# One encoder layer in float32 on one core: the level-16 update of a scan moved into its preparation, 20 column pairs ahead of the scan instead of 19, and another order of loads for the down projection

## The chip, the cores and the metric

The kernel runs on one core of a Trainium2 chip, in one launch. The metric is the device time of the whole program in microseconds (us). Five engines work side by side, each on a queue of its own: TensorE (PE in the profile; its loads of weights are PEld), VectorE (DVE), ScalarE (ACT), GpSimd (POOL) and SyncE (SP), which issues most of the DMA transfers. Matmuls write into PSUM, which holds eight banks of 128x512 float32.

## What is computed

One layer of a bidirectional encoder, batch 1, 1024 positions, model width 1024. The reference, cut to what matters here:

```
proj = einsum("bsd,de->bse", rmsnorm(x), w_in)
glu_in, q, v, z_f, z_b, og, g_a, g_b = split(proj)      # 1024 columns each
a = conv module on glu_in: glu, depthwise conv of 31, layernorm, silu, product with pw_w
o = gated scan forwards (q, v, z_f) + gated scan backwards (q, v, z_b)   # 8 heads of 128
b = (rmsnorm per head(o) * norm_w * silu(og)) @ o_w
x = x + (sigmoid(g_a) * a + sigmoid(g_b) * b) @ w_out
up, val = split(rmsnorm(x) @ w_up)                        # 2816 columns each
x = x + (silu(dwconv3(up)) * val) @ w_down
out = rmsnorm(x)
```

The scan of one head is S_t = diag(f_t) S_(t-1) + k_t v_t^T, o_t = S_t^T q_t, in float32, with f = lb + (1 - lb) sigmoid(z) and k = 1 - f.

## The kernel before

**Products.** Every product in float32 is made of three matmuls of two-part operands: the operand is copied to a rounded high part by ScalarE, the low part is the difference, by VectorE (`split`, L122 to L128), and `mm3` (L146 to L150) issues high x high, high x low, low x high. Weights come as raw tiles `wr` or `sw` and are split to `wp` or `wq`. A *standard job* (`std_job`) makes a column block of 128 for two halves of 512 positions; it gives control back after every six matmuls, one *piece*. A *pair job* (`pair_job`) takes two column blocks together as a 2x2 block product in seven products instead of eight, Winograd's form, with sums of weights and of activations made by VectorE or by adding DMAs; a pair has 14 pieces. Evictions `su` keep products for later sums; in the down projection they are made on L1805.

**Order.** TensorE's instructions run in the order in which the program issues them. For the other engines a planner that works with its own costs chooses the order, except for instructions that are pinned (`pin`), which stay in program order. DMA issues of SyncE stand in one queue, so a load whose tile is not free yet holds up the loads behind it. Streams of work are interleaved by hand: `fill(n)` issues n pieces of a stream, fractions being carried over.

**Ahead of the scan.** The first NPAIRS = 19 pairs of the 28 in the list `todo` (q, og, then v, z forwards and z backwards of each head, then the two gates) are pair jobs. They are issued between the 124 steps of the depthwise convolution (CONV_FILL pieces a step), then between the parts of the layer norm (fixed numbers of pieces), and what is left is drained. The columns that remain are standard jobs in the stream `dense`, with the product with pw_w behind them; their last pieces fill the scan.

**The scan** goes through 16 half heads (8 heads, two halves of 512 positions). Within 32 positions it works by levels of 1, 2, 4, 8 and 16: at each level the keys kG and the queries qF are copied out (`woven`, L1170 to L1175, ScalarE, into one of 8 rotating buffers `A`), and then kG and qF are multiplied in place by the decay of the level (`double_keys` and `double_queries`, through `tt` on L1142, VectorE), and the totals `tb` are combined. `scan_base` prepares a half head in five steps up to level 8, and copies out A16; its last step was empty. `scan_levels` then issues the matmuls of levels 8 and 16 into one bank (L1193; level 16 reads qF itself by a view of two runs of 16), doubles for 16, and merges the results into D by masked copies (L1294). Next come the blocks of 32 (L1276, behind a zeroing with `none`, L1298), the doubling for 32, the blocks of 64, and the copy of the result to S, onto which four DMAs from ScalarE's queue put D (L1306). `scan_states` turns kG (L1316), copies it out as kT (L1318, ScalarE) and multiplies it with v (L1325). `scan_outputs` of the head before runs meanwhile as `pending`.

After each of these five parts `between(FILL)` is called: FILL = 1.77 pieces of the dense stream, one step of the next half head's preparation, and one step of the pending outputs. That is 80 calls in all.

**The down projection** treats the first 6 column tiles of the gated activations by standard jobs (48 pieces), then 12 by two blocks of seven-product jobs, and the last 4 by standard jobs. Their tiles are loaded by `load_part` into seven landing tiles (`ev` and `tm`), issued on L1758, and split four pieces later into buffers of high and low parts (`hx` and `gx`), pinned. The first 12 loads come in the last pieces of the stage before. For the first seven-product block, 12 loads come early, and nine in the pieces -2 to +6 around its start; their buffers are those of the first tiles.

Of the kernel before, what the change touches and what calls it, by code (L numbers as in the profile page):

```python
# [16 lines left out]
AX = mybir.AxisListType  # L17

P = 128
FILL = 1.77  # L20
TAIL = ((1, 2), (1, 1), (2, 4), (2, 3))
CONV_FILL = 1.67
NPAIRS = 19
LN_FILL = 6
LN_LAST = 12
GLU_FIRST = 4
# [5 lines left out]
H = 512  # L32
# [5 lines left out]
def view(t, off, dims):  # L38

    return bass.AP(  # L40
        tensor=t.tensor,
        offset=t.offset + off,
        ap=[list(t.ap[0])] + [list(d) for d in dims],
    )
# [3 lines left out]
def tile_hybrid_encoder(  # L48
# [201 lines left out]
    def std_job(src, nk, acts, evac, halves=(0, 1), step=2):  # L250


        def prep():
            raw = raw_w(src, nk)
            return split(w_page(nk), w_page(nk), raw, V)

        def run(w, halves=halves):
            for half in halves:
                acc = bank("mm")
                for k in range(nk):  # L260
                    mm3(acc, w, acts(k, half), k, k == 0, k == nk - 1)
                    if k % step == step - 1 or k == nk - 1:
                        yield
                evac(half, acc)

        return prep, run
# [306 lines left out]
    FIRST, NS, SEVENS = 6, 3, 2  # L573
# [254 lines left out]
    def in_pair(n):  # L828
        (c0, e0), (c1, e1) = todo[2 * n], todo[2 * n + 1]
        evs = (e0, e1)  # L830
        return pair_job(
            in_cols(c0),
            in_cols(c1),
            NK2,
            lambda i: ht[i],
            p1,
            p1,
            lambda e, *quadrant: evs[e](*quadrant),
            first=n == 0 or n >= 14,
            columns=2,  # L840
        )
# [179 lines left out]

    jobs = collections.deque(in_pair(n) for n in range(1, NPAIRS))
    jobs.appendleft((lambda: w_pair0, pair0[1]))
# [20 lines left out]
    for _ in conv_steps():  # L1044
        s_pairs.fill(CONV_FILL)

# [39 lines left out]

    rest = todo[2 * NPAIRS :]
    rest_jobs = [std_job(in_cols(c), ND, h_std, e) for c, e in rest[:-2]]
# [78 lines left out]
    def pairs(t, h, other=H):  # L1167

        return view(t, 0, [[other + h, 2], [2 * h, H // (2 * h)], [1, h]])

    def woven(t, h):

        t_h = page(hp, "A", 8)
        A.copy(pairs(t_h, h, 0), pairs(t, h))  # L1174
        return t_h  # L1175

    def slot(b, n):
        return b[:, n * P : (n + 1) * P]
# [12 lines left out]
    def level(b, A_t, Q_t):  # L1191
        for at, g, o in each():
            T.matmul(b[g, o], A_t[:, at : at + 32], Q_t(at), start=True, stop=True)  # L1193

    def row(t):
        return lambda at: t[:, at : at + 32]

    def double_keys(kG, tb, h):
        n, nb = H // (2 * h), H // h
        tt(pairs(kG, h), pairs(kG, h), view(tb, 1, [[nb - 1, 2], [2, n], [0, h]]))  # L1200

    def double_queries(qF, q, tb, h):
        n, nb = H // (2 * h), H // h
        tt(pairs(qF, h), q, view(tb, nb + 1, [[-(nb + 1), 2], [2, n], [0, h]]))

    def totals(tb, h, to=None):
        n, nb = H // (2 * h), H // h
        tn = None
        if to is None:
            tn = hp.tile([P, 2, n], F32, tag=f"tb{h}", name=nm("tb"), bufs=1 if h < 8 else 2)  # L1210
            to = view(tn, 0, [[n, 2], [1, n]])
        tt(to, view(tb, 0, [[nb, 2], [2, n]]), view(tb, 1, [[nb, 2], [2, n]]))
        return tn

    def scan_base(ins):


        q, f, kG, ks = ins
        qF = hp.tile([P, 2, H], F32, tag="qF", name=nm("qF"), bufs=4)
        D_t = hp.tile([P, 4, 32], F32, tag="D", name=nm("D"), bufs=3)  # L1220
        for d in range(2):
            V.tensor_scalar(kG[:, d, :], kG[:, d, :], ks[:, d : d + 1], None, op0=ALU.mult)
        k_d, Q1 = page(hp, "A", 8), page(hp, "A", 8)
        tt(k_d, kG[:, 0, :], kG[:, 1, :], ALU.add)
        A1 = woven(kG, 1)
        odd = H // 2
        tt(
            pairs(Q1, 1, 0),
            view(q, 0, [[1, 2], [2, odd], [1, 1]]),
            view(f, H, [[1 - H, 2], [2, odd], [1, 1]]),  # L1230
        )
        tt(
            view(qF, 1, [[H - 1, 2], [2, odd]]),
            view(q, 1, [[-1, 2], [2, odd]]),
            view(f, H + 1, [[-(H + 1), 2], [2, odd]]),
        )
        double_keys(kG, f, 1)
        double_queries(qF, pairs(Q1, 1, 0), f, 1)
        tb = totals(f, 1)
        yield  # L1240
        A2, Q2 = woven(kG, 2), woven(qF, 2)
        double_keys(kG, tb, 2)
        double_queries(qF, pairs(qF, 2), tb, 2)
        tb = totals(tb, 2)
        A4, Q4 = woven(kG, 4), woven(qF, 4)
        yield
        b = bank("sc")
        for n, (k_t, q_t) in enumerate(((k_d, q), (A1, Q1), (A2, Q2), (A4, Q4))):
            level(slot(b, n), k_t, row(q_t))
        double_keys(kG, tb, 4)  # L1250
        double_queries(qF, pairs(qF, 4), tb, 4)
        tb = totals(tb, 4)
        A8, Q8 = woven(kG, 8), woven(qF, 8)
        yield
        A.copy(D_t, near(slot(b, 3)))
        for n, m in enumerate((m_d, m_1, m_2)):
            V.copy_predicated(D_t, over(m), near(slot(b, n)))
        double_keys(kG, tb, 8)
        double_queries(qF, pairs(qF, 8), tb, 8)
        tb = totals(tb, 8)  # L1260
        A16 = woven(kG, 16)
        yield
        yield qF, kG, tb, D_t, A8, Q8, A16

    def scan_levels(base, S_t, Tt):


        qF, kG, tb, D_t, A8, Q8, A16 = base

        def blocks(b, h):  # L1270

            for c in range(0, H, P):
                for s0 in range(0, P, h):
                    t0 = s0 ^ h
                    d = s0 // h % 2
                    T.matmul(  # L1276
                        b[s0 : s0 + h, c + t0 : c + t0 + h],
                        kG[:, d, c + s0 : c + s0 + h],
                        qF[:, 1 - d, c + t0 : c + t0 + h],
                        start=True,  # L1280
                        stop=True,
                    )

        def double(tb, h, to=None):
            double_keys(kG, tb, h)
            double_queries(qF, pairs(qF, h), tb, h)
            return totals(tb, h, to)

        b = bank("ob")
        level(slot(b, 0), A8, row(Q8))  # L1290
        level(slot(b, 1), A16, lambda at: view(qF, at, [[H + 16, 2], [1, 16]]))
        tb = double(tb, 16)
        for n, m in enumerate((m_8, m_16)):
            V.copy_predicated(D_t, over(m), near(slot(b, n)))  # L1294
        yield
        b = bank("sc")
        for at, g, _ in each():
            T.matmul(b[g, at : at + 32], none, none, start=True, stop=True)  # L1298
        blocks(b, 32)
        tb = double(tb, 32)  # L1300
        yield
        blocks(b, 64)
        double(tb, 64, view(Tt, 0, [[4, 2], [1, 4]]))
        A.copy(S_t, c4(b))
        for g in range(0, P, 32):
            nc.scalar.dma_start(S_t[g : g + 32, :, g : g + 32], D_t[g : g + 32])  # L1306
        yield
# [135 lines left out]
    for h in range(NH):  # L1443
# [4 lines left out]
        for half in range(2):  # L1448
            i = 2 * h + half
            base = cur.result()  # L1450
# [11 lines left out]
            for n, _ in enumerate(scan_levels(base, S_t, Tt[:, half])):  # L1462
                if n == 1:
                    b = bank("tr")
# [3 lines left out]
                    A.copy(v.rearrange("p c e -> p (c e)"), b)  # L1468
                between(FILL)
            qF, kG = base[:2]  # L1470
            for _ in scan_states(i, kG, v, Tt, Sf, Sb):
                between(FILL)
            kept.append((S_t, v, qF))
# [297 lines left out]
        return load_part((f0, i, k), src[i] if i < 4 else d_gc[f][i - 4])  # L1771

    s_ffn.fill(14 * (NF - 1) - s_ffn.count)
    for f in range(FIRST):
        for half in range(2):
            later(4, load_g(f, half))
            s_ffn.fill(1)
    s_ffn.drain()
# [145 lines left out]
    starts = [ND * per_std]  # L1924
# [37 lines left out]
    for s in range(SEVENS):  # L1962
        todo = [(FIRST + 2 * NS * s, i, k) for i in PRODUCTS for k in range(NS)]
        if s == 0:
            at = [12 + 2 * n for n in range(12)] + [starts[0] - 2 + n for n in range(9)]
        else:
            at = [starts[s] - 36 + 6 * n for n in range(NS)]
            at += [
                starts[s] - per_seven - 2 + per_seven // 7 * n + max(0, k - 1)
                for n in range(1, 7)  # L1970
                for k in range(NS)
            ]
        for n, key in zip(at, todo):
            fill_to(n)
            later(4, load_seven(*key))
    n = starts[-1] - per_seven - 12
# [49 lines left out]
```

## Time and profile before

| | before |
|---|---|
| time, median of 3 runs | 1750.13 us (1748.18 to 1753.58) |
| the profiled execution: its time, and its span | 1752.23 us, 1750.4 us |
| granted TensorE clock, mean | 0.997 |
| pairs, with convolution and layer norm | about 118 to 480 us of the span |
| scan | about 504 to 880 us |
| attention output, merge, w_out | about 880 to 1072 us |
| up projection | about 1072 to 1512 us |
| down projection and last norm | about 1512 us to the end |

The time of a run holds what lies around the span of instructions; the profile is of a fourth execution. A line of a group names the source line, the engine, the operation, the tiles as out<-in, their shapes and the count; then busy us, the mean of one in ns, and the idle time of the engine just before these instructions with what ended it. A line of a wait reads: who waited, for whom, us in total, how often, the longest. In a line of time come start, duration, engine, line and operation.

### The profile page before, as it was taken

How to read it: one execution, taken by the hardware profiler on the slowest of the kernel's cores; microseconds unless marked ns; L12 is line 12 of the kernel's file. 1: busy time of each engine (PE TensorE's matmuls, PEld its weight loads, DVE VectorE, ACT ScalarE, POOL GpSimd, SP SyncE). 2: the span in 40 equal slices, each digit the busy share in tenths (PEclk: the TensorE clock that was granted, in tenths of full speed). 3: DMA queues.
4: the chain of work that ended last, by engine and by line, in shares of the span. 5: the costliest groups of instructions: out<-in, count | busy, mean ns of one | idle time of the engine just before them, and what ended most of it. 6: DMA issues, size and time to landing. Idle time of an engine off the chain costs nothing. (4 is left out here: it accounts for less than half of the span.)

```text
span 1750.4 us, 30409 instructions
## 1 busy us (share of the span) xinstructions
PE 1714.9 (98%) x11806; PEld 1409.3 (81%) x11806; DVE 1252.4 (72%) x1919; ACT 819.1 (47%) x1528; POOL 169.9 (10%) x184
## 2 busy tenths in 40 slices
PE   8999999999999999999999999999999999999997
PEld 6878888887888788788878887888887887887775
DVE  5599999746678888788556467676767776647864
ACT  7444433334466677776342245443333434443333
POOL 2201111100000000000000002111111111000110
PEclk9999999999999999999999999999999999999999
DMA  8768888855663344436579466576777876764842
GB/s 288 239 163 186 196 189 193 212 160 167 205 201 109 119 130 125 125 120 199 172 257 329 139 205 192 152 156 150 159 160 158 182 172 147 235 215 145 206 91 97
DMA packets 343750, 308.26 MB, mean 176 GB/s; under 512 B 25262, under 2 KB 255798, under 8 KB 343606
## 3 DMA queue, kind: packets, MB, share of 16 engines
q1 hardware_dynamic: 289590, 267.51, 48.7%
q0 software_dynamic: 44800, 37.76, 14.9%
q10 hardware_dynamic: 9216, 1.05, 0.4%
q8 instruction: 92, 1.51, 0.4%
q14 instruction: 52, 0.43, 0.1%
HBM read 201.40 MB, written 87.03 MB: 165 GB/s over the span
## 5 line engine op out<-in xcount | busy, mean ns | idle before, releaser
L148 PE MATMUL mm<-hx,wp 128*128 128x512 f32 x1068 | 428.0, 401 | 4.9 <-ACT tm L849 2.1
L150 PE MATMUL mm<-hx,wp 128*128 128x512 f32 x1068 | 418.0, 391 | 0.9 <-DVE wp L124 0.9
L149 PE MATMUL mm<-hx,wp 128*128 128x512 f32 x1068 | 417.4, 391 | 0.6 <-DVE hx L124 0.6
L124 ACT CAST wp<-wr 128x1024 fp32r<-128x1024 f32 (+2 forms) x147 | 147.3, 1002 | 263.4 <-PE mm L149 135.7
L148 PEld LDWEIGHTS mm<-hx,wp 128*128 128x128 f32 x1068 | 201.0, 188 | 49.1 <-ACT tm L849 2.5
L150 PEld LDWEIGHTS mm<-hx,wp 128*128 128x128 f32 x1068 | 200.9, 188 | 46.5 <-DVE wp L124 3.7
L149 PEld LDWEIGHTS mm<-hx,wp 128*128 128x128 f32 x1068 | 201.1, 188 | 40.8 <-DVE hx L124 1.5
L124 DVE TENSOR_TENSOR wp<-wr,wp 128x1024 fp32r<-128x1024 f32 (+2 forms) x145 | 169.3, 1168 | 72.5 <-ACT wp L124 71.8
L1037 DVE SCALAR_TENSOR_TENSOR acc<-gl,v_b,acc 128x1024 f32<-128x1024 f32 x120 | 148.8, 1274 | 0.4
L439 ACT COPY su<-mm 128x512 f32<-128x512 f32 x82 | 47.5, 580 | 66.3 <-PE mm L150 66.3
L1142 DVE TENSOR_TENSOR qF<-qF,tb 128x512 f32<-128x512 f32 x96 | 64.9, 684 | 12.1 <-ACT A L1174 12.1
L148 PE MATMUL tr<-hx,wp 128*128 128x512 f32 x180 | 70.5, 392 | 0.0
L124 ACT CAST wq<-sw 128x1024 fp32r<-128x1024 f32 x41 | 43.1, 1052 | 57.7 <-PE mm L149 40.7
L150 PE MATMUL tr<-hx,wp 128*128 128x512 f32 x180 | 70.1, 389 | 0.0
L149 PE MATMUL tr<-hx,wp 128*128 128x512 f32 x180 | 70.0, 389 | 0.0
L1632 DVE SCALAR_TENSOR_TENSOR tm<-gp,v_a,tm 128x512 f32<-128x512 f32 x88 | 65.9, 749 | 4.2 <-ACT tm L1630 2.0
L1142 DVE TENSOR_TENSOR kG<-kG,tb 128x512 f32<-128x512 f32 x96 | 65.4, 684 | 4.1 <-PE sc L1276 4.0
L148 PE MATMUL mm<-hy,wp 128*128 128x512 f32 x164 | 64.5, 393 | 0.0
L149 PE MATMUL mm<-hy,wp 128*128 128x512 f32 x164 | 64.2, 392 | 0.0
L148 PE MATMUL sc<-hy,wq 128*128 128x512 f32 x164 | 64.2, 392 | 0.0
L150 PE MATMUL sc<-hy,wq 128*128 128x512 f32 x164 | 64.2, 391 | 0.0
L149 PE MATMUL sc<-hy,wq 128*128 128x512 f32 x164 | 63.8, 389 | 0.0
(374 smaller groups left out, 3566.9 us busy)
## 6 DMA issues: line engine op xcount, KB each, us to landing
wr<-in_w_in_dram SPq DMA_DIRECT2D x48, 512.0 KB, 4.7
wr<-in_ffn_w_up_dram SPq DMA_DIRECT2D x22, 512.0 KB, 5.6
sw<-in_w_in_dram SPq DMA_DIRECT2D x38, 256.0 KB
d_g<-ft SPq DMA_DIRECT2D x38, 256.0 KB, 2.9
sw<-in_ffn_w_up_dram SPq DMA_DIRECT2D x38, 256.0 KB, 3.4
sw<-in_ffn_w_up_dram POOLq DMA_DIRECT2D x19, 512.0 KB, 8.6
wr<-sw POOLq DMA_DIRECT2D x32, 256.0 KB, 3.4
wr<-wr POOLq DMA_DIRECT2D x32, 256.0 KB, 3.7
```

The lines of the kernel that those rows point to most:

```text
L124: parts = A.copy(hi, src), eng.tensor_tensor(lo, src, hi.bitcast(F32), op=ALU.subtract)
L148: T.matmul(acc, whi[:, k, :], ahi, start=first, stop=False, skip_group_check=again)
L149: T.matmul(acc, whi[:, k, :], alo, start=False, stop=False, skip_group_check=again)
L150: T.matmul(acc, wlo[:, k, :], ahi, start=False, stop=last, skip_group_check=again)
L439: A.copy(t, acc)
L1037: V.scalar_tensor_tensor(acc, g[:, k : k + S], tap(k), acc, op0=ALU.mult, op1=ALU.add)
L1142: V.tensor_tensor(o, a, b, op=op)
L1632: V.scalar_tensor_tensor(c, g[:, o + k : o + k + H], vec("fdw", k * NF + j), c, op0=ALU.mult, op1=ALU.add,)
```

## The change

Three things are changed. A half head's preparation does the doubling of level 16 in its last step, after copying out the queries as Q16, and level 16 reads that copy. The number of pairs goes from 19 to 20, with FILL from 1.77 to 1.56 and CONV_FILL from 1.67 to 1.74. In the down projection, the first 12 tiles are loaded by halves instead of by columns, and the nine later ones of the first seven-product block in the pieces -8 to -3 before its start.

```
-FILL = 1.77
+FILL = 1.56
-CONV_FILL = 1.67
-NPAIRS = 19
+CONV_FILL = 1.74
+NPAIRS = 20
...
-        A16 = woven(kG, 16)
+        A16, Q16 = woven(kG, 16), woven(qF, 16)
         yield
-        yield qF, kG, tb, D_t, A8, Q8, A16
+        double_keys(kG, tb, 16)
+        double_queries(qF, pairs(qF, 16), tb, 16)
+        tb = totals(tb, 16)
+        yield qF, kG, tb, D_t, A8, Q8, A16, Q16
...
-        level(slot(b, 1), A16, lambda at: view(qF, at, [[H + 16, 2], [1, 16]]))
-        tb = double(tb, 16)
+        level(slot(b, 1), A16, row(Q16))
...
-    for f in range(FIRST):
-        for half in range(2):
+    for half in range(2):
+        for f in range(FIRST):
             later(4, load_g(f, half))
             s_ffn.fill(1)
...
-            at = [12 + 2 * n for n in range(12)] + [starts[0] - 2 + n for n in range(9)]
+            at = [12 + 2 * n for n in range(12)] + [starts[0] - 8 + n // 2 for n in range(6)]
+            at += [starts[0] - 5 + n for n in range(3)]
```

More of the change, by code (lines that the diff above doesn't have):

```diff
@@ L1260, in scan_base @@
         tb = totals(tb, 8)
-        A16 = woven(kG, 16)
+        A16, Q16 = woven(kG, 16), woven(qF, 16)
         yield
-        yield qF, kG, tb, D_t, A8, Q8, A16
+        double_keys(kG, tb, 16)
+        double_queries(qF, pairs(qF, 16), tb, 16)
+        tb = totals(tb, 16)
+        yield qF, kG, tb, D_t, A8, Q8, A16, Q16
     def scan_levels(base, S_t, Tt):
-        qF, kG, tb, D_t, A8, Q8, A16 = base
+        qF, kG, tb, D_t, A8, Q8, A16, Q16 = base
         def blocks(b, h):
```

## The prediction, made before the changed kernel ran

> **What bounds the kernel now.** I read the page's busy shares first, then who made TensorE wait, then the scan and the first blocks of the down projection.
>
> ```profile
> span 1750.4 us, 30409 instructions
> PE 1714.9 (98%) x11806; PEld 1409.3 (81%) x11806; DVE 1252.4 (72%) x1919; ACT 819.1 (47%) x1528; POOL 169.9 (10%) x184
> ```
>
> TensorE is busy 98% of the span. Whatever does not shorten TensorE's own list of matmuls or take away one of its waits is worth nothing. The second view lists these waits (total us, how often, longest).
>
> ```profile
> PE sc L1276 <- DVE qF L1142: 4.1, 7, 1.0
> PE sc L1325 <- ACT kT L1318: 2.5, 2, 1.4
> PE mm L656 <- DMA xt<-in_x_dram: 2.4, 1, 2.4
> ...
> PE mm L148 <- DVE su L1805: 1.4, 1, 1.4
> PE mm L150 <- DVE wp L124: 0.9, 2, 0.5
> ...
> PE sc L148 <- DVE su L1805: 0.3, 1, 0.3
> ```
>
> Three of them bear on the change: in the scan the update blocks (L1276) wait for VectorE's qF and the state products (L1325) for ScalarE's copies kT, and in the down projection a product waits for an eviction `su` (L1805). Together they are 4.1 + 2.5 + 1.4 = 8.0 us, 0.5% of the span: no more can be won from waits there. After the first 5 us no wait of TensorE is for a DMA.
>
> **The change part by part.** *Twenty pairs.* The two columns zf and zb of head 7 leave the dense stream. As two standard jobs they are 2 x 2 halves x 8 k x 3 = 96 matmuls of 128x512; as one pair they are 7 products x 4 k x 3 = 84. Twelve go. What one costs on a full TensorE is read where nothing else runs (us of the stretch, PE busy and count):
>
> ```profile
> 340.00:400.00 60.00, 60.00 (x266) 1.00 0.54 155
> ```
>
> 60.00/266 = 0.226 us at a granted clock of 1.00; the times of single matmuls are longer, as they overlap. So 12 x 0.226 = **-2.7 us**. The pair costs VectorE more (three adds on L297, three wide splits and a narrow one, three evictions), on its own stretch of 84 x 0.226 = 19 us:
>
> ```profile
> 330.00:470.00 140.00, 139.25 (x614) 113.71 (x613) 77.74 (x101) 54.04 (x82) 7.55 (x9) 1.00 0.58 170
> ```
>
> Here pairs of the same form run beside the layer norm, with VectorE busy 77.74 of 140 us and ScalarE 54.04, so both hide under TensorE. Without that cover the three adds alone would cost some 2.7 us (four times 128x512, at the 0.68 us of such an instruction in the VectorE rows below). CONV_FILL 1.74 over 124 conv steps issues 8.7 more pieces of the 14 that come; 5.3 stand behind the layer norm. I cost that at nothing.
>
> *Level 16.* Before, the level-16 matmul read qF itself (the view in L1291), so the doubling of qF could start only when that matmul was done, and the blocks of 32 waited for it. One half head in order of time, TensorE first, then VectorE:
>
> ```profile
> 806.35 0.49 PE L1193 MATMUL ob<-qF,A 128*32 128x32 f32 x32
> ...
> 808.36 0.28 PE L1298 MATMUL sc<-none 128*32 128x32 bf16 x16
> 809.64 0.46 PE L1276 MATMUL sc<-qF,kG 128*32 128x32 f32 x32 [1.00 <-DVE qF L1142]
> ```
>
> ```profile
> 807.56 0.69 DVE L1164 TENSOR_SCALAR f<-f 128x1024 f32<-128x1024 f32 x1 [1.41 <-ACT f L1163]
> 808.29 0.69 DVE L1142 TENSOR_TENSOR qF<-q,f 128x512 f32<-128x512 f32 x1
> 808.90 0.68 DVE L1142 TENSOR_TENSOR qF<-qF,tb 128x512 f32<-128x512 f32 x1
> ```
>
> The doubling runs at 808.90, two instructions of the next half head ahead of it, and the blocks start when it ends. With Q16 copied out, both doublings and their totals move into the last step of the preparation, which was empty and lies a whole `between` ahead of the levels. No instruction is added on VectorE, none of the moved ones issues a DMA, and TensorE's matmuls keep their number. The groups by form say how much of L1276 hung on this, and whether the contiguous Q16 reads faster (busy us, mean ns, idle before):
>
> ```profile
> L1276 PE MATMUL sc<-qF,kG 128*64 128x64 f32 x256 | 11.0, 228 | 1.6 <-DVE qF L1142 1.6
> L1193 PE MATMUL ob<-qF,A 128*32 128x32 f32 x512 | 7.8, 199 | 0.0
> L1276 PE MATMUL sc<-qF,kG 128*32 128x32 f32 x512 | 7.4, 198 | 2.5 <-DVE qF L1142 2.5
> L1193 PE MATMUL ob<-A,A 128*32 128x32 f32 x512 | 7.3, 199 | 0.0
> ```
>
> Read in two pieces or in one, a matmul takes 199 ns: nothing there. The blocks of 32 waited 2.5 us and those of 64 waited 1.6; only the first hang on level 16. So **-2.5 us**; bounds: 0 (the planner leaves the doublings late) and -4.1 (less queued on VectorE also frees the 64s).
>
> The price is on ScalarE: one copy per half head.
>
> ```profile
> L1174 ACT COPY A<-qF 128x512 f32<-128x512 f32 x43 | 27.8, 646 | 25.3 <-DMA S<-D 9.3 <-PE sc L1193 7.0 <-DVE qF L1142 5.1
> ```
>
> 16 x 0.646 = 10.3 us of ScalarE. It waits for the doubled qF; behind it in ScalarE's queue stand the copies kT, for which TensorE waits twice already. One of the two, on ScalarE:
>
> ```profile
> 589.74 2.01 ACTq L1306 DMA_DIRECT2D S<-D  x1
> 591.86 0.62 ACT L1174 COPY A<-qF 128x512 f32<-128x512 f32 x1 [4.12 <-DMA S<-D]
> 592.38 0.61 ACT L1174 COPY A<-kG 128x512 f32<-128x512 f32 x1
> ...
> 594.10 0.58 ACT L1318 COPY kT<-tr 128x512 f32<-128x512 f32 x1
> ```
>
> ScalarE was held 4.12 us by the issue of S<-D, then worked off its copies in order, kT last. Q16 comes into just this run. In the 14 half heads without a wait I take it as hidden by the dense pieces; in the two late ones it adds its length: 2 x 0.646 = **+1.3 us** (bounds 0, and 16 x 0.646 = 10.3 if no cover is left). The Trainium skill ("TensorE: Matmul & The Clock Gate", Architectural detail) says that ScalarE and VectorE take instructions strictly first in, first out, and that only TensorE pulls loads of weights ahead. By that rule nothing overtakes a blocked Q16; the row agrees, kT standing 4 us behind a copy that has nothing to do with it, and the rule raises the chance of the third rival.
>
> VectorE's doubling of qF waits in turn for Q16, with the masked copies and the next half head queued behind; a `between` of time lies there. A half head also takes 11 turns of the 8 rotating buffers A instead of 10, so Q2 of the next half head needs the buffer of A8, free only after the levels. I put both at nothing, as the levels never waited (0.0 above); uncovered, a late Q2 costs at most its 0.646 us per half head.
>
> *FILL 1.56.* The scan issues 80 times FILL pieces of six matmuls (6 x 0.226 = 1.36 us): 141.6 before, 124.8 after, for 16 fewer dense pieces. Each `between` covers 0.21 x 1.36 = 0.28 us less. Where a wait stands already it grows by that: 4.1/7 = 0.59 us a wait makes the 1.6 us of the 64s about three, with two at kT five, so 5 x 0.28 = **+1.4 us**. Bounds: 0, and 32 x 0.28 = 9.0 if every block of 64 and every kT lost it. The engines behind these waits have room on average:
>
> ```profile
> 504.00:880.00 376.00, 369.25 (x5869) 310.25 (x5868) 293.20 (x644) 245.70 (x562) 12.83 (x14) 1.00 0.45 138
> ```
>
> VectorE is busy 293 of 376 us (78%) and ScalarE 246 (65%); in 22 us less (16 x 1.36), with Q16 added and none of the dense work's instructions taken off, they come to 83% and 72% at most.
>
> *Down tiles.* VectorE at the start of the first seven-product block:
>
> ```profile
> 1572.08 0.69 DVE L124 TENSOR_TENSOR hx<-tm,hx 128x512 fp32r<-128x512 f32 x1
> ...
> 1573.28 0.68 DVE L124 TENSOR_TENSOR hx<-tm,hx 128x512 fp32r<-128x512 f32 x1
> ...
> 1575.69 0.68 DVE L124 TENSOR_TENSOR hx<-tm,hx 128x512 fp32r<-128x512 f32 x1
> ...
> 1576.76 0.68 DVE L124 TENSOR_TENSOR hx<-ev,hx 128x512 fp32r<-128x512 f32 x1
> 1577.36 0.68 DVE L1805 TENSOR_TENSOR su<-mm,xr 128x512 f32<-128x512 f32 x1
> ```
>
> Four splits of late tiles stand ahead of the `su` for which TensorE waits 1.4 us. About 0.6 us apart, they are 2.4 us; moved off, `su` is in time. The nine loads go from pieces -2 to +6 around the block's start to -8 to -3. Their buffers are those of the first down tiles; loading these half by half makes the first six the ones that half 0 reads, free when its last pass ends. So **-1.4 us**; bounds 0 and -2.2 (all waits for L1805 and wp above, 1.4 + 0.3 + 0.5). Six of the nine are now issued two per piece into seven landing tiles:
>
> ```profile
> SPq L1758 <- DVE hx L124: 38.4, 29, 9.2
> ```
>
> SyncE waits for these tiles 29 times already, up to 9.2 us, with the weights' loads queued behind, and still TensorE never waits for a DMA. I put it at nothing; if one wait like the present `su` comes of it, it costs the 1.4 us again. The twelve reordered loads start the stage in the order of use, where TensorE has no wait now: nothing.
>
> **Sum.** -2.7 - 2.5 - 1.4 + 1.3 + 1.4 = -3.9 us. Against the profiled execution (1752.23 us, span 1750.4) that is 1748.3; it lies 2.1 us above the median of 1750.13, so the forecast as a median is **1746.2 us**, 0.22% faster. A measurement of this kernel tells about 0.3% (5.3 us: under 1744.9 or over 1755.4) from no change.
>
> **Rivals.** *All these waits go.* VectorE, rid of the doublings between levels and blocks, reaches everything in time: -2.7 - (4.1 + 2.5) - 2.2 = -11.5, **1738.6 us**. For it: VectorE has 22% free in the scan. Against it: the kT waits come from the issue of S<-D, which stays.
>
> *The change does not do what it says.* The planner orders VectorE and ScalarE by its own times; it may leave the doublings late and the splits in the way. Then only the twelve matmuls are won, and the thinner cover costs: -2.7 + 1.4 = -1.3, **1748.8 us**. Against it: in the preparation's last step they precede in emission everything of the next half head.
>
> *ScalarE becomes the bound in the scan.* With Q16 in front and a shorter cover, kT is late in every half head as it is in two now: 16 x 1.25 = 20.0 us instead of 2.5, +17.5 - 2.7 - 2.5 - 1.4 = +10.9, **1761 us**, slower. With seven such waits the gain is gone (5 more x 1.25 = 6.3 against 6.6), from twelve on (10 more, 12.5) it is slower by over 0.3%. For it: the queue row above, and four issues of S<-D per half head that do not count as busy. Against it: 65% busy, and only two waits in 16 now.
>
> **How the numbers follow.** Forecast 0.42 (own range 1744 to 1750), all waits go (wholly or by more than half) 0.33, not done 0.13, ScalarE 0.12. Faster by over 0.3%: 0.33 and the low edge of the forecast 0.09, 0.42; within: 0.33 + 0.13 = 0.46; slower: 0.12. The range goes from 1738.6 to 1755: it holds the first three cases and the unknown costs up to +1.3 + 9.0 - 6.6 and one wait, and leaves out most of the ScalarE case and a thin low end.
>
> **What would show it.** 84 matmuls more on L148 to L150 in the pairs and 96 fewer on the standard jobs; L1276 of 32 without idle time, the 64s near 2.4 us; kT near 4.4 us in two or three waits; no wait for L1805 at the first seven-product block. Wrong if kT waits appear in most half heads, if new waits of TensorE name Q16's group (L1193 <- A), or if VectorE's qF still ends at the start of the 32s.

## The result, and the profile after

| | before | after |
|---|---|---|
| time, median of 4 runs | 1749.18 us (1748.18 to 1753.58) | 1772.22 us (1768.87 to 1773.22) |
| ratio to before | | 1.0121 (95% interval 1.0106 to 1.0136) |
| span of the profiled execution, mean clock | 1750.4 us, 0.997 | 1770.0 us, 0.992 |

The changed kernel is 23 us slower; the forecast was 1746.2 us, and the range ended at 1755. The first lines of its page:

```profile
span 1770.0 us, 30404 instructions
...
PE 1718.0 (97%) x11794; PEld 1412.3 (80%) x11794; DVE 1260.2 (71%) x1927; ACT 830.1 (47%) x1546; POOL 170.6 (10%) x184
```

TensorE has the twelve matmuls less that were counted (11806 to 11794), and is busy 3.1 us longer all the same, in a span 19.6 us longer. So the time went into waits, and into matmuls that ran longer. The list of TensorE's waits says where (who waited for whom: us in total, how often, the longest):

```profile
PE mm L148 <- DVE ev L798: 14.0, 6, 4.5
PE sc L1327 <- ACT kT L1320: 4.3, 4, 1.5
PE ob L1368 <- DVE Sb L1420: 3.9, 4, 1.7
PE mm L148 <- DVE ev L1104: 3.0, 1, 3.0
PE sc L1279 <- DVE qF L1142: 2.8, 4, 1.2
...
PE sc L148 <- DVE su L1807: 0.3, 1, 0.3
```

(Lines from 1261 on stand two or three higher than before: L1276 is L1279 now, L1325 is L1327, L1805 is L1807.) The signs that the prediction had named came true, but for one count: kT stands at 4.3 us, in four waits and not in two or three; qF is down to 2.8; no wait is left at the first seven-product block. The largest wait is one for which it had no term: 14.0 us, in the pairs ahead of the scan, for VectorE's eviction on L798. Before, this stretch looked so (waits between 118 and 500 us):

```profile
PE mm L148 <- DVE ev L798: 0.8, 1, 0.8
PE mm L148 <- ACT su L439: 0.7, 1, 0.7
```

The longest of the six, in order of time; TensorE first (start, duration, instruction; in brackets the idle time before it and who ended it), then VectorE:

```profile
495.59 0.39 PE L150 MATMUL sc<-hx,wq 128*128 128x512 f32 x1
500.50 0.79 PE L148 MATMUL mm<-hx,wp 128*128 128x512 f32 x1 [4.52 <-DVE ev L798]
```

```profile
493.79 0.54 DVE L1076 TENSOR_SCALAR cx<-cx,v_a 128x512 f32<-128x512 f32 x1
494.25 1.22 DVE L124 TENSOR_TENSOR wq<-sw,wq 128x1024 fp32r<-128x1024 f32 x1
...
496.44 1.28 DVE L1075 TENSOR_TENSOR cx<-cx,tm 128x512 f32<-128x512 f32 x2
...
498.25 0.68 DVE L124 TENSOR_TENSOR ch<-cx,ch 128x512 fp32r<-128x512 f32 x1
498.85 0.99 DVE L1076 TENSOR_SCALAR cx<-cx,v_a 128x512 f32<-128x512 f32 x2
499.76 0.68 DVE L798 TENSOR_TENSOR ev<-su,mm 128x512 f32<-128x512 f32 x1
```

A pair makes its seven products in the order 1, 2, 6, 7, 5, 4, 3, two pieces each. `sc<-hx,wq` is product 4, `mm<-hx,wp` product 3. Product 3 goes on accumulating in a bank that an eviction on L798 has to read first; between product 5, which this eviction reads, and product 3 lies product 4 alone, 12 matmuls, 2.7 us. Here the layer norm's last block for one half of the positions (L1075, L1076 and the splits `ch` of its result; the split `wq` is of a pair's weights) stands in VectorE's queue ahead of the eviction, more than 5 us of it, and product 3 is 4.5 us late.

The two longest waits, 3.7 and 4.5 us, cost twice. Two views by windows, each the stretch of one of them, then the stretches after it (us, busy time and count of PE, PEld, DVE, ACT, POOL, granted clock, DMA share, GB/s):

```profile
447.00:452.00 5.00, 1.45 (x7) 0.87 (x5) 5.00 (x9) 3.57 (x7) 0.00 (x0) 0.91 0.42 130
452.00:458.00 6.00, 5.85 (x14) 4.59 (x15) 2.53 (x4) 1.54 (x3) 0.00 (x0) 0.50 1.07 398
458.00:464.00 6.00, 6.00 (x28) 4.97 (x27) 1.83 (x2) 2.25 (x4) 0.00 (x0) 1.00 0.85 277
495.00:500.00 5.00, 0.98 (x5) 0.48 (x3) 5.00 (x10) 2.86 (x7) 0.00 (x0) 0.89 0.55 196
500.00:506.00 6.00, 5.50 (x13) 4.32 (x14) 2.34 (x4) 2.01 (x5) 0.12 (x1) 0.52 0.84 318
506.00:512.00 6.00, 6.00 (x28) 4.94 (x27) 1.71 (x2) 2.48 (x4) 0.00 (x0) 1.00 0.37 117
```

In the 6 us behind either wait the granted clock is 0.50 and 0.52, and 14 and 13 matmuls run where the next 6 us hold 28: some 3 us more are lost each time.

### The profile page after: what moved, and what is told of

It is laid out like the page before. It is cut to its first block, busy times and chain, and to the rows that moved or that the text cites. A ratio compares the mean times of both kernels' runs of the same rounds, so it can differ in the third digit from the quotient of the medians.

```text
span 1770.0 us, 30404 instructions
## 1 busy us (share of the span) xinstructions
PE 1718.0 (97%) x11794; PEld 1412.3 (80%) x11794; DVE 1260.2 (71%) x1927; ACT 830.1 (47%) x1546; POOL 170.6 (10%) x184
## 5 line engine op out<-in xcount | busy, mean ns | idle before, releaser
L148 PE MATMUL mm<-hx,wp 128*128 128x512 f32 x1044 | 421.2, 403 | 18.5 <-DVE ev L798 14.0
L150 PE MATMUL mm<-hx,wp 128*128 128x512 f32 x1044 | 410.6, 393 | 1.3 <-DVE wp L124 1.3
L149 PE MATMUL mm<-hx,wp 128*128 128x512 f32 x1044 | 410.3, 393 | 0.0
L148 PEld LDWEIGHTS mm<-hx,wp 128*128 128x128 f32 x1044 | 198.1, 190 | 62.7 <-DVE ev L798 16.8
L150 PEld LDWEIGHTS mm<-hx,wp 128*128 128x128 f32 x1044 | 197.9, 190 | 45.5 <-DVE wp L124 3.0
L149 PEld LDWEIGHTS mm<-hx,wp 128*128 128x128 f32 x1044 | 198.3, 190 | 38.7 <-issue 0.5
L439 ACT COPY su<-mm 128x512 f32<-128x512 f32 x84 | 48.7, 580 | 69.5 <-PE mm L150 69.3
L148 PE MATMUL tr<-hx,wp 128*128 128x512 f32 x184 | 71.8, 390 | 0.0
L149 PE MATMUL tr<-hx,wp 128*128 128x512 f32 x184 | 71.6, 389 | 0.0
L150 PE MATMUL tr<-hx,wp 128*128 128x512 f32 x184 | 71.6, 389 | 0.0
L148 PE MATMUL sc<-hy,wq 128*128 128x512 f32 x168 | 65.8, 392 | 0.0
L150 PE MATMUL sc<-hy,wq 128*128 128x512 f32 x168 | 65.7, 391 | 0.0
L149 PE MATMUL sc<-hy,wq 128*128 128x512 f32 x168 | 65.3, 389 | 0.0
```

The source lines that it names most:

```text
L148: T.matmul(acc, whi[:, k, :], ahi, start=first, stop=False, skip_group_check=again)
L149: T.matmul(acc, whi[:, k, :], alo, start=False, stop=False, skip_group_check=again)
L150: T.matmul(acc, wlo[:, k, :], ahi, start=False, stop=last, skip_group_check=again)
L439: A.copy(t, acc)
```

## The experiments

Five theories were tried. **A, the phase:** CONV_FILL 1.74 moves the layer norm's bursts on VectorE to a bad place within a pair. **B:** the twentieth pair is dear in itself. **C:** the reordering of level 16 and of the loads costs. **D, the cover:** FILL 1.56 lengthens the scan's waits. **E:** the copy Q16 makes kT late. Ratios are to before on the same chip, with 95% intervals; medians in us.

**The phase, undone in two ways.** A count of pieces predicts it. In before, the convolution issues 124 x 1.67 = 207.1 pieces, the layer norm 6 + 6 + 5 = 17 up to its last block: 224.1 = 16 pairs of 14 and 0.1; the second half comes 29 pieces later, at 1.1 of a pair. After: 124 x 1.74 + 17 = 232.8, at 8.8 of a pair, and at 9.8: within product 5 (8 to 10), whose eviction product 3 (12 to 14) waits for. First, the changed kernel with the old CONV_FILL:

```
-CONV_FILL = 1.74
+CONV_FILL = 1.67
```

> The changed kernel with CONV_FILL back at 1.67 (20 pairs, FILL 1.56, level 16 and the down loads as changed). Theory A (phase): 1.74 moved the layer norm's bursts on VectorE to the piece of a pair at which product 3 needs the eviction ev (L798); counted in pieces, the first burst stands at 207.1 + 17 = 224.1, 0.1 into a pair of 14, before, and at 232.8, 8.8 into a pair, in the changed kernel. With 1.67 it stands at 0.1 again: TensorE's waits for ev fall from 14.0 us to about 1 us, the halved clock behind three of them goes, and the time falls by about 20 us to 1750 to 1753 us. Theory B (the pair): the twentieth pair itself, with its adds, fills VectorE; the waits stay near 14 us and the time near 1770. Theory C (level 16 or the down loads reorder VectorE in the pairs as well): also near 1770.

Measured: 1756.51 us (1751.92 to 1759.58), ratio 1.0041 (1.0025 to 1.0058); 15.7 us under after. Its waits between 118 and 525 us:

```profile
PE mm L148 <- ACT su L439: 1.0, 1, 1.0
PE mm L148 <- DVE ev L798: 0.7, 1, 0.7
```

The 14.0 us are 0.7 again. The scan starts at 523.4 us of the span, 19.0 later than before, which is exactly the twentieth pair's 84 x 0.226; in after it starts at 544.0. Of these 20.6 us, 12.3 are idle time of TensorE (from 118 us to the scan it is idle 14.1 us in after, 1.9 us here) and 8.3 are busy time, which the halved clock adds: 411.9 us against 403.6 for the same work, at a mean granted clock of 0.98 against 1.00. Second, the changed kernel with CONV_FILL left at 1.74 and five pieces put between convolution and layer norm, so that the bursts come at 13.8 and 0.8 of a pair:

```
+    s_pairs.fill(5)
     for half in range(2):
         xs = []
```

> The changed kernel with CONV_FILL 1.74, and five more pieces of the pairs issued between the convolution and the layer norm. The bursts move from 8.8 and 9.8 pieces into a pair to 13.8 and 0.8; the convolution's steps are spaced as in the changed kernel. Theory A: the two waits in the layer norm (3.7 and 4.5 us, with about 5 us of halved clock behind them) go, those inside the convolution (1.6, 1.3 and 2.8 us, with some 2 us of halved clock) stay: some 13 us faster than the changed kernel, 1757 to 1761 us. If only the spacing of the convolution's steps mattered, or the twentieth pair, the time stays at 1770 or above.

Measured: 1758.49 us (1757.64 to 1759.49), ratio 1.0059 (1.0044 to 1.0074); 13.7 us under after. One line of its waits between 118 and 525 us:

```profile
PE mm L148 <- DVE ev L798: 4.8, 5, 2.4
```

Five short waits are left. Four of them, 4.5 us, stand inside the convolution (188 to 330 us), ahead of the five pieces, and after has four there too, 5.8 us: they come with the spacing of its steps at 1.74, not from the place of the layer norm. The fifth, behind the convolution, is 0.3 us. The two long ones in the layer norm are gone.

**Each part alone.** The level-16 part of the diff, put into before and nothing else; then the two down loads, put into before and nothing else:

```
+        A16, Q16 = woven(kG, 16), woven(qF, 16)
...
-    for f in range(FIRST):
-        for half in range(2):
+    for half in range(2):
+        for f in range(FIRST):
```

> The kernel before with the level-16 update alone (19 pairs, FILL 1.77, CONV_FILL 1.67, loads as before). By the prediction's terms the 2.5 us of waits of the 32 blocks go and kT costs up to 1.3 us more: 1747 to 1749 us, with no wait for ev in the pairs. Theory C expects waits for ev here and 1755 us or more. A rival for the scan (ScalarE, kT late everywhere) expects over 1755 with kT waits of 10 us or more.

> The kernel before with the two changes of the down loads alone. By the prediction's term, the wait for su of 1.4 us at the first seven-product block goes: 1747.5 to 1749 us, a difference within the noise, seen in the waits of the profile. Theory C expects no waits in the pairs to change here either; a rival (landing tiles hold the queue) expects new waits of 1 us or more in the down projection.

Measured, level 16: 1744.34 us (1742.76 to 1747.48), ratio 0.9979 (0.9969 to 0.9988). In its scan, the groups by form (busy us, mean ns, idle before):

```profile
L1327 PE MATMUL sc<-v,kT 128*128 128x128 f32 x128 | 17.0, 275 | 0.5 <-ACT kT L1320 0.5
L1279 PE MATMUL sc<-qF,kG 128*64 128x64 f32 x256 | 11.0, 228 | 2.0 <-DVE qF L1142 1.9
L1279 PE MATMUL sc<-qF,kG 128*32 128x32 f32 x512 | 7.5, 198 | 0.0
L1193 PE MATMUL ob<-A,A 128*32 128x32 f32 x1024 | 12.2, 199 | 0.0
```

The 32s wait no more (2.5 to 0.0), level 16 itself waits for nothing, the 64s wait about as before (1.6 to 1.9), and kT, which was to grow, fell from 2.5 to 0.5. Measured, down loads: 1747.21 us (1745.3 to 1748.93), ratio 0.9993 (0.9984 to 1.0003): one us, not to be told from nothing, though the profile shows the wait gone (between 1510 and 1700 us):

```profile
PE mm L148 <- ACT gx L124: 0.6, 1, 0.6
...
PE sc L148 <- DVE su L1805: 0.3, 1, 0.3
```

The other waits there are those of before: gx has 0.6 us in both, and another wait for `su`, after 1600 us, 0.3. Neither part costs anything: C is refuted. Both together, in before:

> The kernel before with the level-16 update and the down loads, without the twentieth pair and its two fill numbers (19 pairs, FILL 1.77, CONV_FILL 1.67). If the parts add up, 1748.3 - 3.9 - 1.0 = 1743.3 us, and the whole loss of the change sits in the pairs with their fill numbers. If the parts only gain while they stand alone, 1746 us or more.

Measured: 1743.84 us (1740.72 to 1745.86), ratio 0.9970 (0.9960 to 0.9980); kT waits 1.3 us here. This is the version that beats both kernels: the change without its pairs.

**The pair part alone,** and the phase from the other side:

```
-FILL = 1.77
-NPAIRS = 19
+FILL = 1.56
+NPAIRS = 20
...
+    s_pairs.fill(8.7)          (second kernel only, ahead of the layer norm)
```

> The kernel before with 20 pairs and FILL 1.56, CONV_FILL kept at 1.67, without the level-16 update and with the down loads as before. Theory D (cover): FILL 1.56 alone costs the scan, through less time between an update and its use; then the scan shows more waits of TensorE than the 11.2 us with level 16 moved, the 32 blocks' among them (some 15 us), and the time is 1758 to 1764 us. Theory E (Q16): it is the new ScalarE copy that makes kT and Sb late under the thin cover; then the scan shows 9 us of waits or less here, and the time is 1750 to 1755 us.

> As the 20 pairs with CONV_FILL 1.67 and nothing else, with 8.7 more pieces of the pairs issued between the convolution and the layer norm, so that the layer norm's bursts stand 8.8 and 9.8 pieces into a pair as in the changed kernel, while the convolution's steps are spaced as before. Theory A (phase): the two waits for ev in the layer norm come back, 8 us with some 5 us of halved clock, and the time is 11 to 15 us above the same kernel without the shift. If only CONV_FILL's spacing made them, there is no difference.

Measured: pairs and FILL alone 1755.6 us (1754.73 to 1760.08), ratio 1.0045 (1.0031 to 1.0059); with the 8.7 pieces 1769.45 us (1769.05 to 1771.23), ratio 1.0121 (1.0105 to 1.0136). In the scan of the first the waits are 11.8 us, between the some 15 that D foresaw and the 9 or less of E, so this run does not decide between these two. The shift alone costs 13.9 us, and brings the waits back (118 to 525 us):

```profile
PE mm L148 <- DVE ev L798: 9.3, 3, 4.5
```

No conv step is spaced otherwise here, and of the three waits two are those of after, 3.7 and 4.5 us in the layer norm: A holds for the place within the pair. Last, the changed kernel with a CONV_FILL that lands the bursts one whole pair later, at 124 x 1.783 + 17 = 238.1, 0.1 into a pair:

```
-CONV_FILL = 1.74
+CONV_FILL = 1.783
```

> The changed kernel with CONV_FILL 1.783, which gives the convolution 14 pieces more than 1.67, one whole pair: the layer norm's bursts stand at 0.1 and 1.1 pieces into a pair again, one pair later. Theory A: no long waits for ev in the layer norm, as with 1.67, and about the same time, 1753 to 1758 us; waits inside the convolution may remain (1 to 5 us in all). If a larger CONV_FILL as such were bad, it is worse than 1.74, over 1772 us.

Measured: 1759.27 us (1753.53 to 1761.72), ratio 1.0047 (1.0031 to 1.0063), as with 1.67. Its largest waits:

```profile
PE ob L1368 <- DVE Sb L1420: 3.9, 4, 1.7
PE sc L1327 <- ACT kT L1320: 3.3, 4, 1.1
PE mm L148 <- DVE ev L798: 3.0, 3, 1.6
```

So more pieces per conv step are not what hurts: 1.67 and 1.783 are alike, and 1.74 between them is 13 to 16 us slower.

**Where the rest lies.** Without the phase the pair part still costs, while twelve matmuls fewer should win. FILL was moved alone, in before and in the version with both reorderings; with 19 pairs the matmuls are the same, and the pieces that the scan does not take run behind it:

```
-FILL = 1.77
+FILL = 1.56
```

> The kernel before with FILL 1.56 alone: TensorE has the same matmuls as before, 17 dense pieces move from inside the scan to its end. Theory D (cover): inside the scan TensorE waits some 10 to 12 us instead of 6.6 us, and the pieces at the end hide little that was not hidden: 1753 to 1758 us. Rival (the loss with 20 pairs is the twentieth pair's): no change, 1748 to 1750 us. The first prediction's term for the thinner cover was +1.4 us.

> The level-16 update and the down loads with 19 pairs, and FILL 1.56. Theory D: the waits for kT, Sb and qF of the 64 blocks come up to about 11 us as they did with 20 pairs; 6 to 10 us above the same kernel with FILL 1.77 (1743.8), 1750 to 1754 us. If the update moved into the preparation makes the scan insensitive to its cover, 1744 to 1746 us.

Measured: in before 1760.76 us (1759.78 to 1764.65), ratio 1.0065 (1.0046 to 1.0084); with the reorderings 1759.85 us (1755.81 to 1764.31), ratio 1.0060 (1.0041 to 1.0079). Both are slower than even theory D had expected. With before, the seven kernels form a table of ratios:

| | 19 pairs, FILL 1.77 | 19 pairs, 1.56 | 20 pairs, 1.56 | 20 pairs, 1.56, CONV_FILL 1.74 |
|---|---|---|---|---|
| old preparation and loads | 1 | 1.0065 | 1.0045 | |
| new | 0.9970 | 1.0060 | 1.0041 | 1.0121 |

Read along a row, the thinner cover costs 0.65% (11 us) or 0.90% (16 us), the twentieth pair wins 0.2% (3 us, no more than the uncertainty of one such step) in both, and the phase costs 0.8% (14 us; the small waits within the convolution are in it, and the shift alone cost 13.9). Read down a column, the reordering wins 0.3% with the old cover and nothing that can be told with the thin one. B is refuted: the pair costs nothing. D holds.

What the thin cover does in the scan of before (window from the scan's first matmul to its last output, then the stretch up to the next stage; the first line is before, the other two FILL 1.56, one fence for each kernel):

```profile
504.40:878.20 373.80, 367.05 (x5860) 308.70 (x5859) 292.66 (x642) 243.87 (x555) 12.83 (x14) 1.00 0.44 137
```

```profile
505.40:864.60 359.20, 347.87 (x5758) 292.55 (x5757) 285.26 (x630) 241.10 (x551) 12.84 (x14) 0.99 0.41 126
864.60:997.90 133.30, 129.13 (x566) 105.74 (x565) 72.12 (x104) 36.15 (x63) 1.83 (x2) 0.99 0.80 249
```

102 matmuls, 17 pieces, left the scan. At 0.226 us they are 23.1 us; the scan became only 14.6 shorter, so 8.5 were lost there, 4.6 of them as idle time (373.80 - 367.05 = 6.75 before, 359.20 - 347.87 = 11.33 now), the other 3.9 in TensorE's busy time. Most of that is clock, behind two waits of 1.85 and 1.99 us that end at 624 and 649 us:

```profile
625.40:629.40 4.00, 4.00 (x13) 3.07 (x12) 3.92 (x7) 2.18 (x4) 0.00 (x0) 0.57 0.12 45
649.40:653.40 4.00, 4.00 (x22) 3.88 (x23) 2.10 (x5) 0.22 (x1) 0.00 (x0) 0.57 0.00 0
```

At 0.57 each of these 4 us does the work of 2.3, so some 3.4 us go there; before has no such stretch in its scan, and neither has the profile with the reorderings. Behind the scan the same pieces took 27.0 us instead of 23.1 (the stretch there was 106.3 us before); 2.8 of these 3.9 us are idle time, with the waits for `ev` on L1104 (4.17 us idle now, 1.40 before). Waits from 500 to 905 us, first FILL 1.56 in before, then with the reorderings; those for `ev` on L1104 lie behind the scan:

```profile
PE sc L1276 <- DVE qF L1142: 8.3, 9, 1.9
PE mm L148 <- DVE ev L1104: 3.3, 2, 2.5
PE ob L1366 <- DVE Sb L1418: 2.6, 2, 2.0
PE sc L1325 <- ACT kT L1318: 0.4, 1, 0.4
```

```profile
PE mm L148 <- DVE ev L1104: 4.1, 3, 2.2
PE ob L1368 <- DVE Sb L1420: 4.0, 4, 1.7
PE sc L1279 <- DVE qF L1142: 3.3, 4, 1.4
PE sc L1327 <- ACT kT L1320: 2.8, 4, 1.3
```

Under the thin cover kT is late with Q16 (2.8 here, 4.2 with twenty pairs) and hardly without it (0.4); under the old cover Q16 does not make it later (2.5 us in before, 0.5 and 1.3 with Q16): E is a matter of cover, and of 2 to 4 us. And a wait that neither before nor the best version has stands in every kernel with FILL 1.56 whose scan is shown here: products of the pending outputs (L1366 or L1368) wait for the chain of states Sb on VectorE. In after, at one of them:

```profile
682.27 0.35 DVE L1420 SCALAR_TENSOR_TENSOR Sb<-Sb,Tt,Sb 128x128 f32<-128x128 f32 x1
682.53 0.68 DVE L1142 TENSOR_TENSOR kG<-kG,tb 128x512 f32<-128x512 f32 x1
683.13 0.34 DVE L1420 SCALAR_TENSOR_TENSOR Sb<-Sb,Tt 128x128 f32<-128x128 f32 x1
683.40 0.68 DVE L1142 TENSOR_TENSOR qF<-qF,tb 128x512 f32<-128x512 f32 x1
```

VectorE alternates between the chain and the next half head's doublings, so a link of the chain comes every 0.86 us, two and a half times its own 0.34.

**Buying the cover back,** with twenty pairs, and beyond, with eighteen:

```
-FILL = 1.56               (after, with CONV_FILL 1.67)
+FILL = 1.77
...
-NPAIRS = 19               (before with both reorderings)
-FILL = 1.77
-CONV_FILL = 1.67
+NPAIRS = 18
+FILL = 1.98
+CONV_FILL = 1.557
```

> The changed kernel with CONV_FILL 1.67 and FILL 1.77: 20 pairs, level 16 and the down loads as changed, the old cover in the scan, with the dense pieces running out about one half head before its end. Theory D: the scan's waits for qF, kT and Sb fall from 11.2 us to 3 us or less while the pieces last, and some waits come at the end of the scan: 1744 to 1751 us. Theory E: waits for kT and Sb stay above 6 us although the cover is back.

> The level-16 update and the down loads, one pair fewer than before (18), FILL 1.98 and CONV_FILL 1.557, which keep the layer norm's phase. Twelve matmuls more, +2.7 us; the scan's waits that are left with FILL 1.77 (3.3 us) can at most go. Theory D: the cover is already enough at 1.77, so 1743 to 1747 us, no better than 19 pairs. If cover is still short at 1.77 in ways that the waits do not show, under 1742 us.

Measured: twenty pairs with FILL 1.77 1755.33 us (1753.14 to 1756.54), ratio 1.0037 (1.0023 to 1.0051), no better than 1.0041. The pieces end before the scan does, and its last part stands bare:

```profile
PE tr L1394 <- ACT tm L1387: 4.8, 1, 4.8
PE ob L1368 <- DVE Sb L1420: 3.2, 1, 3.2
```

Eighteen pairs with FILL 1.98: 1754.45 us (1752.04 to 1757.3), ratio 1.0025 (1.0013 to 1.0037), where 1743 to 1747 us had been expected. Its scan:

```profile
495.40:884.50 389.10, 389.10 (x5961) 328.34 (x5961) 296.91 (x645) 258.03 (x577) 12.83 (x14) 1.00 0.45 138
```

TensorE is busy 389.10 of 389.10 us: with this cover no wait is left in the scan. The kernel is slower than with 19 pairs nonetheless, and the pairs say why (100 to 500 us):

```profile
PE mm L148 <- DVE ev L798: 6.7, 3, 3.6
```

By the count the layer norm stands at 0.1 of a pair again (124 x 1.557 + 17 = 210.1), and no wait for `ev` is there. The three end at 174, 312 and 352 us: with 1.557 pieces to a conv step the collision came at other places, at the first with five conv steps in a row (6.09 us), two splits and a sixth step ahead of the eviction on VectorE. So the count says where the layer norm falls, and nothing of the convolution's own steps. Waits in the pairs can hide what a cover wins, so this run does not say what 18 pairs could do.

## Why the prediction was wrong

**The step that failed** is this: "CONV_FILL 1.74 over 124 conv steps issues 8.7 more pieces of the 14 that come; 5.3 stand behind the layer norm. I cost that at nothing." The count was right, and it holds the answer: 8.7 pieces are 0.62 of a pair, so everything on VectorE that is tied to the convolution's end moves by 0.62 of a pair against the pairs' own evictions. It cost 15.7 us by medians, 0.8% by ratios. The pair's VectorE work was said to hide under TensorE because VectorE was busy 77.74 of 140 us; a mean share says nothing of a burst that stands ahead of an eviction with 2.7 us of cover.

**The mis-sized term** is FILL: +1.4 us, with bounds 0 and 9.0. It measured +11 in before and about +16 with the reorderings. The bounds came from waits already in the list, each grown by 0.28 us. But waits that had been covered appeared (Sb in the scan, `ev` on L1104 behind it), the clock fell behind two of the waits, and the pieces cost 27.0 us behind the scan against 23.1. A list of waits shows what sticks out of the cover, not what lies just under it.

**The terms that held.** *Twelve matmuls*, -2.7: the table gives 0.2%, about -3.3 us, in both rows, which agrees and is too small to be measured by one step. *Level 16*: the 32s' 2.5 us went, as worked out; together with the loads -5.2 us by the ratio, where -2.5 - 1.4 + 1.3 = -2.6 was the sum. The difference is kT: its +1.3 had the wrong sign with the old cover (2.5 to 0.5, and to 1.3 with the loads, so -1.2), and came out with the thin one (2.8 to 4.3 us in all). *Down loads*, -1.4: about -1.0, inside its bounds and not to be told from nothing.

**The sum.** With the ratios of the table on 1749.2 us: -5.2 for the reorderings, +15.7 for FILL, -3.3 for the pair, +14.0 for the phase, together +21.2: the 1.0121 measured. This adds up by construction, since each term is a step in the table; each step carries some 0.2%, 3 to 4 us, of uncertainty. How much falls to FILL and how much to the pair depends on which of the two steps is taken first: in the row of before, 3.9 us of FILL's price arose behind the scan, where with twenty pairs the pieces do not run. Their sum, +12.4 us here, does not depend on it.

**The rivals.** *All waits go*: no; though in the scan with FILL 1.98 they did. *The change does not do what it says*: it does. *ScalarE the bound*, 1761 us: right only in that the kernel is slower. kT waits in four half heads, not sixteen, for 4.3 us and not 20. The rule cited there, from the Trainium skill ("TensorE: Matmul & The Clock Gate", Architectural detail), that VectorE and ScalarE take instructions strictly in order, bears on the case after all, but on the other engine, and the trace agrees: the eviction that starts at 499.76 could have run from 493.3 on, when product 5 was done, and stood behind the layer norm's instructions. (The 4 us that the prediction counts from a copy to kT are those from the issue of S<-D at 589.74; from the copy of A at 591.86 it is 2.2 us.)

**What stays open.** The spread of the kernels with FILL 1.56 (7.7 us in the first experiment, 8.5 with the reorderings and 19 pairs, whose profile is one of its two fastest runs). That after's scan begins 20.6 us behind that of the first experiment, of which 14 to 16 arrive in the time: the first experiment's profile lost some of it again further on, with 2.8 us of waits for `su` (L439) in the up projection; the rest was not traced. How the small waits inside the convolution divide between its steps was not tried.

## What to carry to other kernels

Work that is woven in by hand as filler is also the cover of the stage that it fills: taking some of it away, be it to run it cheaper, costs what was hidden under it, and a list of waits does not show this. A ratio of interleaving sets the phase of one stream's bursts against the other stream's repeating pattern; count both in the same unit, reduce by the length of the pattern, and look at what the burst now stands ahead of. A mean busy share of 55% excuses no queue: compare the longest burst with the shortest cover.

## What the runs showed of the hardware

Idle time of TensorE can be paid for again in clock. Behind after's wait of 2.79 us at 305.6 us:

```profile
309.00:314.00 5.00, 5.00 (x13) 3.98 (x12) 4.96 (x6) 0.51 (x1) 0.18 (x1) 0.50 0.78 239
...
920.50:926.00 5.50, 5.47 (x24) 4.59 (x25) 4.09 (x6) 1.22 (x4) 0.00 (x0) 1.00 0.87 279
```

The clock is 0.50 for 5 us. The second line follows a wait of 2.97 us (at 917.56, the one for `ev` on L1104), and there it stays at 1.00. In before, 2.10 us at 95 us sufficed for a clock of 0.66 over 97 to 102 us, and with FILL 1.56 the 1.85 us before 624 for 0.57 over 4 us. The Trainium skill ("TensorE: Matmul & The Clock Gate", Part 1) has the clock fall to half when TensorE is idle over a window of some 3.4 us. The halves of these rows agree with its half speed. The length of the idle time alone does not decide here: 1.85 us, shorter than that window, sufficed once, and 2.97 us did not.
